# The output projection of a gated mixer as seven block products, with the modulation sums and some weight splits moved

## The chip, the cores and the metric

The kernel runs on one core of a Trainium2 chip. Its metric is the device time of one execution in microseconds, the median of several. The engines are TensorE (PE in the profile, PEld its weight loads), VectorE (DVE), ScalarE (ACT), GpSimd (POOL) and SyncE (SP, which here only issues DMAs). Each runs its own instruction stream in order; semaphores join them.

## The reference, cut to what matters

```python
mod = silu(c) @ w_ada + b_ada                       # six vectors of 1024
sh1, sc1, g1, sh2, sc2, g2 = split(mod, 6)
h = rms_norm(x, norm_mix_g) * (1 + sc1) + sh1
b_s, c_s, v_s, v_c, gl_c, gate_br = split(h @ w_in)
y_a = (b_s * causal_dwconv3(c_s * v_s)) @ w_short_out              # mixer A
u = silu(layer_norm(causal_dwconv31(v_c * sigmoid(gl_c)) + b))
y_b = u @ w_conf_out                                               # mixer B
g_a, g_b = split(sigmoid(gate_br), 2)
mix = (g_a * y_a + g_b * y_b) @ w_o                                # the output projection
x = x + g1 * mix
h2 = rms_norm(x, norm_ffn_g) * (1 + sc2) + sh2
a, bgate = split(h2 @ w_ffn_in, 2)
x = x + g2 * ((silu(a) * bgate) @ w_ffn_out)
return rms_norm(x, final_norm_g)
```

x is 1024 tokens by 1024 channels in float32, the ffn 2816 wide.

## The kernel before

Everything is held transposed: a tile has 128 channels on the partitions and 512 tokens (a "half", `H`) along the row; eight such blocks (`KC`) are the model width. Float32 products are made in three passes: each operand is split into a high part, rounded to the matmul's input form (`copy` on ScalarE), and a low part (the difference, on VectorE or GpSimd); `mm3` then issues high x high, high x low and low x high. For a weight block of 128 x 1024, `split_w` makes both parts (`wh`, `wl`); its argument `lo_engine` says which engine makes the low one.

All large products but one are made by a seven-product block scheme (Winograd's form of Strassen's): the matrices are cut two by two, in channels of the input, pairs of output blocks and halves of the tokens, and `PRODUCTS = "1265734"` names the seven products in the order in which their results can be summed in PSUM. A unit (`dual`) has four output blocks. `product` issues one product of a dual: two PSUM banks, four row blocks, three passes, 24 matmuls. Its operands are sums of blocks: of the activations (made by VectorE and split again) and of the weights (made by VectorE, by GpSimd, or by a DMA that adds into SBUF, `accum_op`).

The stages in order: the first projection with the short convolution and the long one of 31 taps (VectorE's `conv`, whose taps are laid between the evacuations); mixer A's projection (`ya_order`); mixer B's (`CONF_ORDER`), after its layer norm; the output projection `mix`; the ffn in (`in_order`); the ffn out. Weights come through a list `plan`; `next_w` keeps `AHEAD = 2` more loaded and split than the product that is being issued. The order of the instructions on an engine is worked out when the kernel is built, by a planner that goes by costs of its own; `tc.issue_after(ins)` puts an instruction behind another on its engine.

The output projection alone is plain. Weights are whole output columns, `w_o[k]`; for each half, all eight outputs are made one after the other, each with eight row blocks (`col_block`). `mg` holds the split merged activations, `mg_split(j, h)`. Each result is multiplied by g1 and added to x (`scalar_tensor_tensor`, line 1471), stored to DRAM for later (`x1_dram`), squared on ScalarE (1475) and summed (1481). After half 0, `norm_2_first` makes its norm and the eight operands of the ffn's products 1 and 2 (`h2_of`), while half 1 is projected. The second half's norm (`norm_2_start`) is taken in the middle of the ffn's first product, and `norm_2_half` makes its operands beside the next four.

The modulation vectors are 48 sums, each over a block of `w_ada` of 128 x 1024, by one VectorE instruction (`modulation_of`, line 486). Sixteen are made at the start. Of the other 32, fourteen lie in the first projection, two in each of seven duals, through weight buffers; ten are made beside the output projection, by `load_b`; eight beside the ffn.

```python
        for n in range('55'.count(m) * (BEGUN < d < GATED)):
            with tc.issue_after(short_conv.ins):
                modulation_of(MOD_FROM + n_mod, load(ada[MOD_FROM + n_mod], home=...))
```

The second ffn dual, `in_units[1]`, is begun early: `begin` loads its blocks and makes two sums of them (lines 278 and 284) during the output projection, at the places `S2_AT`.

Of the kernel before, what the change touches and what calls it, by code (L numbers as in the profile page):

```python
# [38 lines left out]
ALU = mybir.AluOpType  # L39
# [48 lines left out]

AHEAD = 2


S2_AT = (2, 3, 4)

# [46 lines left out]
def block_kernel(ctx: ExitStack, tc: tile.TileContext, x0, xT, c, vecs, ada, w_first, w_plain, w_duals,  # L140
# [26 lines left out]
    ucp, diffp = (p for _, p in phase_1)  # L167
    rawbp = pool("raw_b", 2, side="right")

    def ps_tile(name):  # L170
# [80 lines left out]
    def dual_units(mats, n, early=0, eng=nc.vector):  # L251
# [20 lines left out]
        def begin():  # L272

            with tc.issue_after(load.ins):
                get("21", "22")
            yield
            with tc.issue_after(parts.lo):
                eng.tensor_tensor(a["22"], a["21"], a["22"], ALU.add)
            with tc.issue_after(load.ins):
                get("11")  # L280
            yield
            a["s2"] = s2p.tile([P, T], F32, tag="x1", name="s2")[:, :n]
            with tc.issue_after(mix.half_0):
                eng.tensor_tensor(a["s2"], a["11"], a["22"], ALU.add)
            yield

        def unit_begun(m):
            get(*{"1": ("11",), "2": ("12",), "5": ("21", "22"), "7": ("11", "12"), "4": ("22",)}.get(m, ()))
            if m == "5":
                sums("1")  # L290
            elif m == "7":
                sums("3")
                eng.tensor_tensor(a["12"], a["12"], a["s2"], ALU.add)
            return split_w(a[{"1": "11", "2": "12", "6": "s2", "5": "s1", "7": "21", "3": "12", "4": "22"}[m]], n, (), eng)
# [61 lines left out]
    def added_units(mats):  # L356
# [9 lines left out]
        def unit(m):  # L366
# [10 lines left out]
            else:  # L377
                raw = a["s1"] if m == "5" else load(mat[{"1": "11", "2": "12", "4": "22"}[m]])
            return split_w(raw, 1024)

        return {m: (lambda m=m: unit(m)) for m in PRODUCTS}

    conf_homes, conf_adds = [rawp, rawbp, rawp], []

    def conf_units(mats, d):
# [15 lines left out]
        def unit(m):  # L401
# [11 lines left out]
            else:  # L413
                raw = get({"1": "11", "2": "12", "4": "22"}[m])
            return split_w(raw, 1024, () if m in "12" else (split.act, split.ins))

# [45 lines left out]
    plan += [yb_units[d][m] for d, m in yb_order]  # L462
    plan += [(w_o[k], 1024) for ks in (range(KC), SECOND[KEPT:]) for k in ks]
    ready = []
# [778 lines left out]
    win_evacs = begun + [win_evac(d, PAIRS[2 * d : 2 * d + 2], win_banks[d]) for d in range(BEGUN, n_duals)]  # L1243
    n_mod = 0
    for d, m in win_order:
# [20 lines left out]
        if win_order.index((d, m)) >= len(win_order) - 7:  # L1266
            q_steps.pop(0)()
        for n in range('55'.count(m) * (BEGUN < d < GATED)):
            with tc.issue_after(short_conv.ins):
                modulation_of(MOD_FROM + n_mod, load(ada[MOD_FROM + n_mod], home=(dual_units.home,dual_units.home)[n_mod % 2]))  # L1270
            n_mod += 1
    while late:
        late.pop(0)()

    tz = {m: [None] * KH for m in PRODUCTS}
# [35 lines left out]

    def load_b(i):

        loaded.append((i, load(ada[i])))
        if len(loaded) > 1:
            with tc.issue_after(split.ins):
                modulation_of(*loaded.pop(0))


    for j in range(KC):  # L1320
        conv(j)
        add_conv(j)
    ma = {}
    loaded = []

# [44 lines left out]
    for i, (d, m) in enumerate(ya_order):  # L1370
        gates_a(d, m)
        product(ya_banks[d], m, tq[m], ya_evacs[d], onto="2")
        if q_steps:
# [12 lines left out]
    mg = [[None, None] for _ in range(KC)]  # L1386

    def mg_split(o, h):
        mg[o][h] = split(ma[o, h], hl_tile, f"mg{o}{h}")

    def yb_evac(d, banks):
# [3 lines left out]
        def out(i, row, h, op, src):  # L1395
# [3 lines left out]
            if (row, h) == (1, 0):  # L1399
                nc.vector.tensor_tensor(ma[j, h], ma[j, h], g, ALU.add)  # L1400
                mg_split(j, h)
            else:
                nc.gpsimd.dma_start(ma[j, h], g, accum_op=ALU.add)
# [38 lines left out]
    def z_3(k):  # L1442
# [5 lines left out]
        (0, "6"): each(z_3, *range(KH)), (1, "6"): each(z_7, *range(KH)), (0, "3"): each(z_4, *range(KH)),  # L1448
        (0, "4"): lambda: [mg_split(j, 0) for j in range(0, KC, 2)],
    }  # L1450
    for d, m in yb_order:
# [4 lines left out]
        product(yb_banks[d], m, tz[m], yb_evacs[d], onto="2", by_k=m in "12")  # L1456
        z_steps.get((d, m), lambda: None)()


    x1 = [None] * KC  # L1460
    x1_dram = [dram.tile([P, T], F32, name=f"x1_dram{j}") for j in range(KC)]

    def mix(i, h):
        j = SECOND[i] if h else i
        xr = g_tile("xr")
        nc.gpsimd.dma_start(xr, xT[j, :, halves[h]])
        (o,) = col_block((second_w if h else first_w)(i), mg, (h,), "mix", SECOND if h else [*range(0, KC, 2), *range(1, KC, 2)])
        if h == 0:
            x1[j] = ucp.tile([P, T + CK - 1], F32, tag="uc", name=f"x1{j}")[:, :T]
        dst = x1[j][:, halves[h]]  # L1470
        evac = nc.vector.scalar_tensor_tensor(out=dst, in0=o, scalar=modc(16 + j), in1=xr, op0=ALU.mult, op1=ALU.add)
        if (i, h) == (KC - 1, 0):
            mix.half_0 = evac.ins
        nc.gpsimd.dma_start(x1_dram[j][:, halves[h]], dst)
        sq = nc.scalar.activation(xr, dst, AF.Square, scale=1.0 / 32.0)
        if (i, h) == (KC - 1, 1):
            load_rsqrt(sq.ins)
        if i == 0:
            sums[h] = xr
        else:  # L1480
            mix.add = nc.vector.tensor_tensor(sums[h], sums[h], xr, ALU.add).ins

    def h2_of(k, h, r2, hi_lo=None):
# [3 lines left out]
        if hi_lo:  # L1487
            hi, lo = hi_lo
            nc.scalar.activation(hi, t, AF.Identity, bias=modc(24 + k))
            nc.vector.scalar_tensor_tensor(  # L1490
                out=lo, in0=t, scalar=modc(24 + k), in1=f32(hi), op0=ALU.add, op1=ALU.subtract
            )
        nc.scalar.activation(t, t, AF.Identity, bias=modc(24 + k))
# [4 lines left out]
    def norm_2_first():  # L1498

        ss, hl = ps_tile("ss"), parts(sums[0])  # L1500
        load_rsqrt(parts.ins)
# [40 lines left out]
    in_units = [dual_units([w_fi[d, m] for m in range(4)], 1024, EARLY[d]) for d in range(N_IN)]  # L1542
    close(phase_1.pop())
    s2p = open_pool("s2", 1, side="right", stack=ctx)[1]
    sums = {}
    for h in range(2):
        for i in range(KC):
            mix(i, h)
            if h == 0:
                mg_split(i, 1)  # L1550
                for b in [32 + i] + [MOD_FROM + n_mod + i] * (MOD_FROM + n_mod + i < 32):
                    load_b(b)
            if (h, i) == (0, KC - 1):
                modulation_of(*loaded.pop())
            if h == 1 and i == 0:
                for k in range(KC):
                    affine(aff2, k, 32, vec, V_GFFN)
                norm_2_first()
            if h == 1 and i in S2_AT:
                next(in_units[1]["begin"])  # L1560


    in_order = [(0, "1"), (0, "2"), (1, "1"), (1, "2"), (2, "1")] + [(d, m) for d in range(2) for m in PRODUCTS[2:]]
# [16 lines left out]

    plan += [lambda d=d, m=m: in_unit(d, m) for d, m in in_order]
    ha = {}
    in_banks = [{} for _ in range(N_IN)]
# [108 lines left out]

    in_product(0, "1", norm_2_start)
    r2 = rstd_end(*r2)
    for i, (d, m) in enumerate(in_order[1:5]):
        norm_2_half(i, r2)
        in_product(d, m)
# [308 lines left out]
```

## Time and profile before

| what | us |
|---|---|
| median of 3 runs (1442.38 to 1443.21) | 1442.85 |
| the profiled execution | 1443.7 |
| its span, first to last instruction | 1441.9 |
| TensorE busy | 1428.6 |
| VectorE busy | 1198.8 |
| ScalarE busy | 655.2 |
| GpSimd busy | 522.0 |

The profile gives, for one execution, the busy time of each engine, the chain of work that ended last, the costliest groups of instructions, and, asked by stretch of time, the busy time of each engine in each stretch. A group's row reads: line, engine, operation, output<-inputs by the program's names, shapes, count | busy us, mean ns of one | idle time ahead of them and what ended it. A row of the timeline begins with its start and its duration in us, and may stand for several like instructions in a row (x4).

### The profile page before, as it was taken

How to read it: one execution, taken by the hardware profiler on the slowest of the kernel's cores; microseconds unless marked ns; L12 is line 12 of the kernel's file. 1: busy time of each engine (PE TensorE's matmuls, PEld its weight loads, DVE VectorE, ACT ScalarE, POOL GpSimd, SP SyncE). 2: the span in 40 equal slices, each digit the busy share in tenths (PEclk: the TensorE clock that was granted, in tenths of full speed). 3: DMA queues.
4: the chain of work that ended last, by engine and by line, in shares of the span. 5: the costliest groups of instructions: out<-in, count | busy, mean ns of one | idle time of the engine just before them, and what ended most of it. 6: DMA issues, size and time to landing. Idle time of an engine off the chain costs nothing.

```text
span 1441.9 us, 17770 instructions
## 1 busy us (share of the span) xinstructions
PE 1428.6 (99%) x6322; PEld 1173.5 (81%) x6322; DVE 1198.8 (83%) x1665; ACT 655.2 (45%) x963; POOL 522.0 (36%) x512
## 2 busy tenths in 40 slices
PE   8999999999999999999999999999999999999997
PEld 4888888888888888888888888888888888888887
DVE  7996999999899999989988898877777665866676
ACT  4873333333343457567426474533444443321235
POOL 0017777777677562013311001110111015563405
PEclk9999999999999999999999999999999999999999
DMA  9743233333335578768886248645555449996903
GB/s 349 282 162 90 72 117 117 103 117 103 132 124 183 161 244 296 219 193 203 223 317 228 79 141 267 205 149 186 185 175 161 138 143 358 389 372 191 340 0 117
DMA packets 95946, 275.04 MB, mean 191 GB/s; under 512 B 10945, under 2 KB 12993, under 8 KB 95858
## 3 DMA queue, kind: packets, MB, share of 16 engines
q1 hardware_dynamic: 46672, 148.92, 30.6%
q0 software_dynamic: 44000, 111.36, 25.6%
q10 hardware_dynamic: 5186, 13.64, 2.5%
q8 instruction: 49, 0.80, 0.2%
q14 instruction: 39, 0.32, 0.1%
HBM read 203.09 MB, written 67.63 MB: 188 GB/s over the span
## 4 chain that ended last, share of the span: by engine, by line
PE 97%; POOL 1%; DVE 0%; issue 0%; POOLq 0%
PE bank L506 14%; PE bank L505 14%; PE bank L508 14%; PE x L508 8%; PE x L506 8%; PE x L505 8%; PE z L506 4%; PE z L508 4%; PE z L505 4%; PE y L508 3%; PE y L506 3%; PE y L505 3%; PE mix L506 2%; PE mix L508 2%; PE mix L505 2%; PE lead L501 1%
## 5 line engine op out<-in xcount | busy, mean ns | idle before, releaser
L244 ACT CAST wh<-raw 128x1024 fp32r<-128x1024 f32 (+2 forms) x254 | 263.0, 1037 | 394.7 <-PE bank L506 138.1
L245 DVE TENSOR_TENSOR wl<-raw,wh 128x1024 fp32r<-128x1024 f32 (+2 forms) x176 | 212.4, 1208 | 38.1 <-ACT wh L244 35.5
L245 POOL TENSOR_TENSOR wl<-raw,wh 128x1024 fp32r<-128x1024 f32 x78 | 194.4, 2500 | 91.1 <-ACT wh L244 90.1
L1168 DVE SCALAR_TENSOR_TENSOR c<-diff,vec,c 128x512 f32<-128x512 f32 x232 | 163.4, 749 | 1.5
L1644 POOL DMA_DIRECT2D hid<-stage x70 | 37.4, 535 | 343.3 <-DVE stage L554 326.8
L505 PE MATMUL bank<-th,wh 128*128 128x512 f32 x336 | 130.7, 389 | 0.0
L506 PE MATMUL bank<-tl,wh 128*128 128x512 f32 x336 | 130.7, 389 | 0.0
L508 PE MATMUL bank<-th,wl 128*128 128x512 f32 x336 | 130.7, 389 | 0.0
L505 PEld LDWEIGHTS bank<-th,wh 128*128 128x128 f32 x336 | 63.1, 188 | 13.2
L508 PEld LDWEIGHTS bank<-th,wl 128*128 128x128 f32 x336 | 63.1, 188 | 13.1
L506 PEld LDWEIGHTS bank<-tl,wh 128*128 128x128 f32 x336 | 63.1, 188 | 13.0
L553 ACT CAST stage<-g 128x512 fp32r<-128x512 f32 x60 | 37.3, 622 | 74.7 <-DMA hid<-stage 41.0
L506 PE MATMUL x<-tl,wh 128*128 128x512 f32 x176 | 68.5, 389 | 0.0
L505 PE MATMUL x<-th,wh 128*128 128x512 f32 x176 | 68.5, 389 | 0.0
L508 PE MATMUL x<-th,wl 128*128 128x512 f32 x176 | 68.4, 390 | 0.0
L1168 DVE SCALAR_TENSOR_TENSOR c<-u,wsum,c 128x512 f32<-128x512 f32 x96 | 66.8, 750 | 0.8
L554 DVE TENSOR_TENSOR stage<-g,stage 128x512 fp32r<-128x512 f32 x60 | 41.2, 688 | 27.9 <-ACT stage L553 27.7
L1668 POOL DMA_DIRECT2D th<-hid x77 | 41.1, 534 | 52.2 <-PE x L508 26.4
L1668 POOL DMA_DIRECT2D tl<-hid x77 | 41.2, 535 | 19.6 <-DMA tl<-hid 5.6
L265 DVE TENSOR_TENSOR raw<-raw 128x1024 f32<-128x1024 f32 (+1 forms) x15 | 17.8, 1188 | 36.4 <-DMA raw<-in_w_fi 24.1
L486 DVE CUSTOM_DVE_ANT_0 raw<-raw,cs,vec 128x1024 f32<-128x1024 f32 x24 | 39.1, 1639 | 9.5 <-DMA raw<-in_ada 5.4
L505 PE MATMUL bank<-t2h,wh 128*128 128x512 f32 x112 | 43.6, 389 | 0.0
(833 smaller groups left out, 4143.1 us busy)
## 6 DMA issues: line engine op xcount, KB each, us to landing
hid<-stage POOLq DMA_DIRECT2D x70, 512.0 KB, 4.8
raw<-in_w_duals SPq DMA_DIRECT2D x65, 512.0 KB, 3.6
raw<-in_w_fi SPq DMA_DIRECT2D x54, 512.0 KB, 4.3
th<-hid POOLq DMA_DIRECT2D x77, 256.0 KB, 6.0
tl<-hid POOLq DMA_DIRECT2D x77, 256.0 KB, 6.0
ada<-in_ada SPq DMA_DIRECT2D x24, 512.0 KB, 5.9
raw<-in_ada SPq DMA_DIRECT2D x24, 512.0 KB, 4.7
raw<-in_w_fo SPq DMA_DIRECT2D x16, 512.0 KB, 6.1
```

Source lines behind the costliest of these rows:

```text
L244: hi = nc.scalar.copy(wh, raw)
L245: lo = lo_engine.tensor_tensor(wl, raw, f32(wh), ALU.subtract)
L265: eng.tensor_tensor(a["s1"], a["21"], a["22"], ALU.add)
L486: nc.vector.tensor_tensor_reduce(out=raw, in0=raw, in1=cs, scale=1.0, scalar=col(V_ADA, b), op0=ALU.mult, op1=ALU.add, accum_out=modc(b),)
L505: nc.tensor.matmul(ps, wh, xh, start=first, stop=False, skip_group_check=again)
L506: nc.tensor.matmul(ps, wh, xl, start=False, stop=False, skip_group_check=again)
L508: mm3.ins = nc.tensor.matmul(ps, wl, xh, start=False, stop=last, skip_group_check=again).ins
L553: t_split.act = nc.scalar.copy(hi, src).ins
L554: t_split.ins = nc.vector.tensor_tensor(lo, src, f32(hi), ALU.subtract).ins
L1168: tap.ins = nc.vector.scalar_tensor_tensor(out=out, in0=src[:, s : s + H], scalar=wt, in1=acc, op0=ALU.mult, op1=ALU.add).ins
L1644: nc.gpsimd.dma_start(hid_dram[key], s)
L1668: nc.gpsimd.dma_start(t, hid_dram[key][:, s])
```

## The change

Five things change together.

1. The output projection is made by seven block products for each of two duals, in the order `MIX_ORDER`. Its weights are loaded as blocks (`mix_units`), sums of blocks by adding DMAs on GpSimd's queue. Its operands are block sums of the merged activations (`m_6`, `m_7`, `m_4`) and plain blocks, split by `tm_split`. Evacuations add g1 times a product, or minus that, into x1. Mixer B's order `CONF_ORDER` is changed so that the blocks needed first come first.
2. With it, `norm_2_first` is issued between the two banks of product 5 of the second dual; `norm_2_start` after the ffn's second product; `norm_2_half` goes with three products instead of four. Shifts of the first half's operands (`shift_2`) go behind the second norm's start.
3. The fourteen modulation sums of the first projection become 28 half sums, one every third product, through a half-size buffer of their own. The next ten leave the output projection: one in every two products of mixer A and B, through the buffer of the convolution's differences.
4. Low parts of weights on GpSimd instead of VectorE: products 1, 2, 4 and 5 of mixer B (`LO_POOL`), and products 1 and 2 of the first three ffn duals.
5. The two sums of `begin` go to GpSimd, at other places (`S2_AT`); of the second half's sums of squares, some.

```diff
-S2_AT = (2, 3, 4)
+LO_POOL = {"ya": "", "yb": "1245", "mix": ""}
+S2_AT = (0, "5"), (1, "5"), (0, "3")
-CONF_ORDER = [(d, m) for m in "1256" for d in range(2)] + [(0, "3")] + [(d, m) for m in "74" for d in range(2)] + [(1, "3")]
-MOD_FROM = 16
+CONF_ORDER = [(d, m) for m in "1256" for d in range(2)] + [(0, "3"), (0, "7"), (0, "4"), (1, "7"), (1, "4"), (1, "3")]
+MIX_ORDER = [(d, m) for m in "1267453" for d in range(2)]
+MOD_FROM, MOD_WIN, MOD_LAST, MOD_EVERY = 16, 14, 24, 3
...
         def begin():
-            with tc.issue_after(parts.lo):
-                eng.tensor_tensor(a["22"], a["21"], a["22"], ALU.add)
+            nc.gpsimd.tensor_tensor(a["22"], a["21"], a["22"], ALU.add)
...
-            with tc.issue_after(mix.half_0):
-                eng.tensor_tensor(a["s2"], a["11"], a["22"], ALU.add)
+            nc.gpsimd.tensor_tensor(a["s2"], a["11"], a["22"], ALU.add)
...
-                w = split_w(a["1" + m], n, (), eng)
+                w = split_w(a["1" + m], n, (), nc.gpsimd if early else eng)
...
+    def mix_units(mats, d):
+        def add(raw, b):
+            conf_adds.append(nc.gpsimd.dma_start(raw, mat[b], accum_op=ALU.add).ins)
+        def unit(m):
+            if m == "6":
+                raw = a["s2"] = get("11", "21", "22", home=(rawp, rawbp)[d])
+            elif m == "3":
+                raw = a["s2"]
+                add(raw, "12")
+            else:
+                raw = get(*{"1": ("11",), "2": ("12",), "7": ("21", "11"), "4": ("22",), "5": ("22", "21")}[m])
+            return split_w(raw, 1024, (split.act, split.ins), lo_engine("mix", m))
...
+    def half_modulation(behind, every=1):
+        n_step += 1
+        if n_step % every or n_mod >= 2 * MOD_WIN:
+            return
+        i, h = n_mod // 2, n_mod % 2
+        with tc.issue_after(load.ins):
+            nc.sync.dma_start(half_ada, ada[MOD_FROM + i][:, halves[h]])
+        n_mod += 1
+        half_sums(i, h, behind)
...
+    def late_modulation(step, behind):
+        if step % 2 == 0:
+            if whole:
+                with tc.issue_after(behind):
+                    modulation_of(MOD_FROM + n_mod, whole.pop())
+                n_mod += 1
+        elif n_mod < MOD_LAST:
+            whole.append(diffp.tile([P, T + CK - 1], F32, tag="diff", name="ada")[:, :T])
+            with tc.issue_after(load.ins):
+                nc.sync.dma_start(whole[0], ada[MOD_FROM + n_mod])
...
+            row, h = {"2": (0, 0), "6": (0, 1), "3": (0, 1), "7": (1, 1), "5": (1, 1), "4": (1, 0)}[m]
+            j = 4 * d + 2 * i + row
+            dst = x1[j][:, halves[h]]
+            src = dst if m in "53" else xrs.pop((j, h))
+            ins = nc.vector.scalar_tensor_tensor(
+                out=dst, in0=ps, scalar=ngm[:, j : j + 1] if row else modc(16 + j), in1=src, op0=ALU.mult, op1=ALU.add
+            ).ins
...
+        steps = {
+            (0, "2"): each(m_6, 0, 1), (1, "2"): each(m_6, 2, 3), (0, "6"): each(m_7, *range(KH)),
+            (1, "6"): each(m_4, *range(KH)), (0, "7"): lambda: [tm_split("5", k, b[0, 0][k]) for k in range(KH)],
+            (0, "4"): lambda: [tm_split("3", k, b[1, 1][k]) for k in range(KH)],
+        }
+        for d, m in MIX_ORDER:
+            xr_loads(d, m)
+            product(banks[d], m, tm[m], evacs[d], norm_2_first if (d, m) == (1, "5") else None, onto="2")
...
-    in_product(0, "1", norm_2_start)
+    in_product(0, "1")
+    in_product(0, "2")
+    with tc.issue_after(mm3.ins):
+        norm_2_start()
```

More of the change, by code (lines that the diff above doesn't have):

```diff
@@ L168, in block_kernel @@
     rawbp = pool("raw_b", 2, side="right")
+    halfp = open_pool("half", 1, side="right")
+    half_ada = halfp[1].tile([P, H], F32, tag="half", name="half_ada")
+    half_sum = halfp[1].tile([P, 1], F32, tag="sum", name="half_sum")
     def ps_tile(name):
@@ L1267, in block_kernel @@
             q_steps.pop(0)()
[L1268 to L1271, printed above, removed]
+        half_modulation(reads[-1][1], MOD_EVERY)
     while late:
         late.pop(0)()
+    assert n_mod == 2 * MOD_WIN, n_mod
+    def late_modulation(step, behind):
+        nonlocal n_mod
+        if step % 2 == 0:
+            if whole:
+                with tc.issue_after(behind):
+                    modulation_of(MOD_FROM + n_mod, whole.pop())
[4 more added lines that the diff above has]
+                nc.sync.dma_start(whole[0], ada[MOD_FROM + n_mod])
+    whole, n_mod = [], MOD_WIN
     tz = {m: [None] * KH for m in PRODUCTS}
@@ L1457, in block_kernel @@
         z_steps.get((d, m), lambda: None)()
+        late_modulation(len(ya_order) + yb_order.index((d, m)), split.ins)
     x1 = [None] * KC
     x1_dram = [dram.tile([P, T], F32, name=f"x1_dram{j}") for j in range(KC)]
[L1463 to L1469, printed above, removed]
+    sums, xrs = {}, {}
@@ L1470, in mix, with xr_loads, x1_done @@
+    def xr_loads(d, m):
+        row, h = {"2": (0, 0), "6": (0, 1), "7": (1, 1), "4": (1, 0)}.get(m, (0, None))
+        for i in range(2 * (h is not None)):
+            j = 4 * d + 2 * i + row
+            xrs[j, h] = g_tile("xr")
+            with tc.issue_after(conf_adds[-1]):
+                nc.gpsimd.dma_start(xrs[j, h], xT[j, :, halves[h]])
+    def x1_done(j, h, sq, ins):
         dst = x1[j][:, halves[h]]
-        evac = nc.vector.scalar_tensor_tensor(out=dst, in0=o, scalar=modc(16 + j), in1=xr, op0=ALU.mult, op1=ALU.add)
@@ L1498, in norm_2_first @@
     def norm_2_first():
-        ss, hl = ps_tile("ss"), parts(sums[0])
+        ss, hl = ring[1][0], parts(sums[0])
         load_rsqrt(parts.ins)
@@ L1542, in block_kernel @@
     in_units = [dual_units([w_fi[d, m] for m in range(4)], 1024, EARLY[d]) for d in range(N_IN)]
-    close(phase_1.pop())
+    close(phase_1.pop(), halfp)
     s2p = open_pool("s2", 1, side="right", stack=ctx)[1]
[L1545 to L1560, printed above, removed]
     in_order = [(0, "1"), (0, "2"), (1, "1"), (1, "2"), (2, "1")] + [(d, m) for d in range(2) for m in PRODUCTS[2:]]
@@ L1581, in block_kernel @@
     plan += [lambda d=d, m=m: in_unit(d, m) for d, m in in_order]
+    ngm = cp.tile([P, KC], F32, name="ngm")
+    nc.vector.tensor_scalar(ngm, mod[:, 16:24], -1.0, None, ALU.mult)
+    for k in range(KC):
+        affine(aff2, k, 32, vec, V_GFFN)
+    for d, m in mix():
+        if (d, m) in S2_AT:
+            next(in_units[1]["begin"])
+    raws[:] = [rawp] * 3 + [rawbp] * 2
     ha = {}
```

125 lines of the change are left out of this document (95 added, 30 removed).

## The prediction

> **What bounds the kernel now.** I read the page's first two parts, then the chain, then the busy times by stage.
>
> ```profile
> span 1441.9 us, 17770 instructions
> PE 1428.6 (99%) x6322; PEld 1173.5 (81%) x6322; DVE 1198.8 (83%) x1665; ACT 655.2 (45%) x963; POOL 522.0 (36%) x512
> PEclk9999999999999999999999999999999999999999
> PE 97%; POOL 1%; DVE 0%; issue 0%; POOLq 0%
> ```
>
> TensorE is busy for 99% of the span at the full granted clock, and the chain that ended last is 97% TensorE. So a matmul that is taken away shortens the run by its own step, as long as nothing else becomes late. The table by stage shows which engine would: short conv and convolution (64 to 561), the two branch projections (564 to 643 mixer A, 643 to 711 mixer B), the output projection (711 to 802), the start of the ffn (802 to 830), and a stretch of plain ffn.
>
> ```profile
> core 0: us, PE busy (x) PEld busy (x) DVE busy (x) ACT busy (x) POOL busy (x), PEclk, DMA share, GB/s
> 64.00:300.00 236.00, 236.00 (x1043) 195.39 (x1042) 211.91 (x307) 105.75 (x153) 150.09 (x78) 1.00 0.34 113
> 300.00:500.00 200.00, 200.00 (x884) 165.62 (x883) 190.01 (x274) 77.84 (x109) 138.15 (x71) 1.00 0.42 140
> 500.00:561.00 61.00, 61.00 (x271) 50.52 (x270) 59.45 (x85) 34.20 (x55) 33.15 (x15) 1.00 0.80 253
> 564.00:643.00 79.00, 79.00 (x349) 64.96 (x348) 69.38 (x101) 45.37 (x68) 8.31 (x11) 1.00 0.78 223
> 643.00:711.00 68.00, 68.00 (x299) 55.55 (x298) 66.02 (x97) 43.45 (x67) 18.57 (x25) 1.00 0.79 196
> 711.00:802.00 91.00, 91.00 (x402) 75.12 (x401) 72.91 (x109) 41.15 (x60) 19.67 (x35) 1.00 0.74 258
> 802.00:830.00 28.00, 28.00 (x123) 22.81 (x123) 24.49 (x33) 14.24 (x21) 0.00 (x0) 1.00 0.22 62
> 900.00:1200.00 300.00, 300.00 (x1325) 248.42 (x1324) 221.20 (x275) 132.71 (x195) 35.76 (x67) 1.00 0.53 173
> ```
>
> TensorE has no gap in any of them. VectorE (DVE) is the second limit: 97% busy in 643 to 711 and 500 to 561, 88% in 564 to 643 and 802 to 830, but only 80% in 711 to 802. GpSimd (POOL) is nearly empty from 564 on.
>
> **The matmuls removed.** The same table restricted to the tile `mix`:
>
> ```profile
> 705.00:806.00 101.00, 87.39 (x384) 72.07 (x384) 12.00 (x16) 1.00 0.75 250
> ```
>
> The projection is 8 outputs x 2 halves x 8 row blocks x 3 passes = 384 matmuls in 87.39 us, 0.2276 us each; the ffn stretch gives 300/1325 = 0.2264. Seven block products are 7 x 2 x 2 x 4 x 3 = 336. So 48 fall away: 48 x 0.2264 = 10.9 us. One product is 24 matmuls, 5.44 us, and the fourteen take 76.2 us. This term is sure; everything else is what of it is lost again.
>
> **VectorE in the new projection.** Durations that I need:
>
> ```profile
> L245 DVE TENSOR_TENSOR wl<-raw,wh 128x1024 fp32r<-128x1024 f32 x14 | 17.1, 1221 | 0.5 <-ACT wh L244 0.3
> L486 DVE CUSTOM_DVE_ANT_0 raw<-raw,cs,vec 128x1024 f32<-128x1024 f32 x10 | 12.7, 1281 | 0.0
> L486 DVE DVE_READ_ACCUMULATOR2_ANT mod<- 128x1 f32 x10 | 0.8, 84 | 0.0
> L1471 DVE SCALAR_TENSOR_TENSOR x<-mix,mod,xr 128x512 f32<-128x512 f32 x16 | 12.0, 750 | 12.3 <-PE mix L508 12.3
> L1481 DVE TENSOR_TENSOR xr<-xr 128x512 f32<-128x512 f32 x14 | 9.6, 689 | 3.0 <-ACT xr L1475 3.0
> 534.15 2.49 DVE L1101 TENSOR_TENSOR q<-q,q1h 128x512 fp32r<-128x512 f32 x4
> ```
>
> The ten modulation sums leave the stage: -10 x (1.28 + 0.08) = -13.6 us. Evacuations go from 16 to 24 (products 2, 6, 7, 4, 5, 3 of two duals and two banks; product 1 goes to ScalarE): +8 x 0.75 = +6.0. Operands: 5 products x 4 splits and 16 block sums, where 8 splits of the second half were before: +28 x 0.62 (four in 2.49 us) = +17.4. One more weight: +1.2. Three sums of squares go to GpSimd: -2.1. The first ffn weights' low parts (three in this stage) and two sums of the begun unit go there too: -5 x 1.22 = -6.1. Together 72.9 + 2.8 = 75.7 us of 80.1 that remain of the 91. It fits, with 4.4 us free instead of 18; the five instructions that move to GpSimd take most of that again if each blocks VectorE for 1 us (below), which is why the edges get a price. ScalarE (41 us plus 12 splits and 4 copies of 0.62, as its cast quoted further down) stays far below. The loads of x and the stores of x1 stay sixteen each.
>
> **The sums moved ahead.** Ten whole sums now lie in 564 to 700, one in two products: six in mixer A's stage, +6 x 1.36 = 8.2 on 69.4 of 79 us: full, but not over. Four lie in mixer B's, +5.4 on 66.0 of 68; eight of that stage's low parts leave VectorE, -8 x 1.22 = -9.8. So by its own work mixer B's stage falls to 61.6. The earlier fourteen become 28 halves, one in three products over the whole first projection. No row shows a half; nearest is a whole one at 1.28, so 0.64 + 0.08 bare, and the blocking below on top. The fourteen take 39.1 - 12.7 = 26.4 us now, 1.89 each:
>
> ```profile
> L486 DVE CUSTOM_DVE_ANT_0 raw<-raw,cs,vec 128x1024 f32<-128x1024 f32 x24 | 39.1, 1639 | 9.5 <-DMA raw<-in_ada 5.4 <-issue 4.0
> 544.38 3.01 POOL L1199 TENSOR_TENSOR tot<-tot,u 128x512 f32<-128x512 f32 x2 [0.72 <-DVE u L1168]
> 560.89 1.88 PE L1208 MATMUL mu<-tot,ones 128*128 128x512 f32 x4
> ```
>
> That is 0.61 above the 1.28. With 0.61 on each half, 28 x 1.33 = 37 us replace 28 us (26.4 and the reads): 9 us more, against 36 us in which VectorE idles from 64 to 561, though the last 60 us have only 1.5. There the cover is another: the channel sums are done at 547.4 and TensorE takes them at 560.9, 13.5 us later. I count 0.5 us for this and mixer A's stage, bounds 0 and 9.
>
> **Low parts on GpSimd.** One costs 2.50 us there for 1.22 on VectorE. The rows in which the two engines meet:
>
> ```profile
> L245 POOL TENSOR_TENSOR wl<-raw,wh 128x1024 fp32r<-128x1024 f32 x78 | 194.4, 2500 | 91.1 <-ACT wh L244 90.1
> L433 DVE TENSOR_TENSOR raw<-raw x4: 3030/3049/3252, 433.7 to 511.9; 128x1024 f32<-128x1024 f32 x4
> L265 DVE TENSOR_TENSOR raw<-raw 128x1024 f32<-128x1024 f32 x13 | 15.9, 1223 | 31.2 <-DMA raw<-in_w_fi 24.1 <-DMA raw<-in_w_fo 7.1
> 534.84 4.08 POOL L245 TENSOR_TENSOR wl<-raw,wh 128x1024 fp32r<-128x1024 f32 x1 [2.28 <-ACT wh L244]
> L1168 DVE SCALAR_TENSOR_TENSOR c<-diff,vec,c 128x512 f32<-128x512 f32 x232 | 163.4, 749 | 1.5
> ```
>
> An add of two SBUF tiles took 3.05 us beside a GpSimd add where the same form takes 1.22 alone: 1.83 of blocking. But in the other direction GpSimd's 2.5 us became 4.08 while VectorE ran its four q splits (534.15, above) back to back; and the taps, one input of which lies in PSUM, keep 749 ns throughout. [...]
>
> So the price hangs on one number, the blocking b that each low part puts on VectorE. Bounds: 0 (GpSimd falls into VectorE's waits and PSUM reads) and 2.5. The nearest rows give 0.61 (sums) and 1.83 (L433); mixer B's stage is mostly SBUF operands, packed closely, which lets GpSimd wait, so I take 1.0. Then the stage has 61.6 + 8 x 1.0 = 69.6 us of VectorE work in 68; some of it has slack before its reader, so I count 1.0 us of stall.
>
> **Edges of the projection.** At its start the last merged block is added by a DMA, 3.2 to 8.2 us to landing; it is first needed by product 6, four products or 21.8 us in:
>
> ```profile
> DMA to landing us min/median/max: 3.2/6.1/8.2
> 757.20 0.62 ACT L682 CAST sumh<-xr 128x512 fp32r<-128x512 f32 x1 [0.76 <-DVE xr L1481]
> 770.62 0.76 DVE L1490 SCALAR_TENSOR_TENSOR h23l<-x,mod,h23h 128x512 fp32r<-128x512 f32 x1
> 801.77 1.12 PE L695 MATMUL ss<-xr,ones 128*128 128x512 f32 x2
> 830.28 0.69 DVE L554 TENSOR_TENSOR t2l<-t,t2h 128x512 fp32r<-128x512 f32 x1 [0.69 <-ACT t2h L553]
> ```
>
> Evacuation 1.5, landing 8.2 and four operands of some 2.5 us make 20: it fits, so nothing. At its end the cover shrinks. The first half's norm, from its cast to the fourth operand, took 771.4 - 757.2 = 14.2 us and had 42 us before the ffn's first product, whose middle the ss row marks (801.8 - 2.7 - 757.2); now it starts in the middle of the twelfth product, with 2.5 products or 13.6 us left. The second half's norm took 801.8 to 831.0, five products; it now starts after the second ffn product, with three (16.3 us) and what product 6 gives before it reads the last operand. Its bare VectorE work is 8 x 0.75 + 12 x 0.69 + 2.1 = 16.4 us; low parts that stood between go to GpSimd. Late next would be that fourth operand. I count 2.0 us for both places, bounds 0 (the freed VectorE time covers it) and 8 (16.4 + 1.8 until the root is there + 2 x 0.69 and 2 x 1.22 of other VectorE work + 2 x 1.0 of blocking = 24, against 16.3, if product 6 gave nothing); nearer to 0, since five such products show no TensorE gap today with VectorE at 88%.
>
> **Transfers.**
>
> ```profile
> L398 POOL DMA_DIRECT2D raw<-in_w_conf x6 | 5.7, 944 | 46.0 <-DVE rl0t L570 19.8 <-DVE z2l L546 11.3 <-DVE bank L867 8.6
> ```
>
> Blocks are loaded 22 times (10 of them added by GpSimd's queue) instead of 13: +4.7 MB in the stage, while ten modulation blocks, 5.2 MB, leave it. Mixer A's stage takes 3.1 MB on 17.6 (223 GB/s x 79 us): share 0.78 to some 0.92. Weights are fetched two products (10.9 us) ahead, which hides a late landing; a stage over 1.0 would not be hidden. SyncE's queue carries the moved loads in turn; nothing else waits on it. GpSimd issues 10 more accumulating DMAs of 0.94 us as in the row, beside 20 us busy of 91; behind them on its queue wait the loads of x, needed only by an evacuation of the same product. I count 0.
>
> **Sum.** -10.9 + 0.5 + 1.0 + 2.0 = -7.4. The profiled execution took 1443.7 (span 1441.9 and 1.8 around it): 1436.3. The median shown, 1442.85, is 0.85 below it, so 1435.5.
>
> **Rivals.**
> - *All of it comes out:* VectorE's freed time covers every edge. For it: not one gap in today's stages at 97% VectorE. 1443.7 - 10.9 - 0.85 = 1432.
> - *VectorE becomes the bound:* b is 1.83 as in L433. Mixer B's stage: 61.6 + 14.6 = 76.2 in 68, 8.2 lost; the edges lose their 2: 1442.85 - 10.9 + 10.2 = 1442. Against it: GpSimd's 4.08 us row, where it was GpSimd that waited.
> - *The low parts on GpSimd make it slower:* b is the whole 2.5. Mixer B's stage then holds 61.6 + 20 = 81.6 in 68, 13.6 us lost: 1442.85 - 10.9 + 13.6 = 1445.6, 1447.6 with the edges. It decides from b = (68 + 10.9 - 61.6)/8 = 2.16 on, or 1.9 with the edges' 2 us. Only L433 comes near.
>
> **How the numbers follow.** Runs of this kernel differ by 0.06%; about 0.2% (2.9 us) is what can be told from no change. Forecast, one to seven us of stalls, 1433 to 1439: 0.57. All of it out: 0.15. VectorE the bound: 0.15. Slower: 0.13. The first two are faster, 0.72; the third the same, 0.15; the last slower, 0.13. The range leaves out a tenth on either side: 1431.5 to 1445. The likeliest case's own range is 1433 to 1439.
>
> **What would show it.** 336 matmuls of the projection where 384 were; VectorE's share over 90% in it; VectorE adds of two SBUF tiles longer than 1.3 us between 620 and 720 only where a GpSimd low part runs (b is their excess per low part); TensorE gaps at the start of the ffn, released by h2 or t2 operands. Wrong it would be if TensorE waits in the first projection (for half sums or late evacuations), or for a merged block at product 6.

## The result, and the profile after

The changed kernel takes 1487.06 us (median of 4 runs, 1484.26 to 1489.74) against 1442.99 before: ratio 1.0306, 95% interval 1.0286 to 1.0325. It is 44 us slower, where 7.4 us faster was predicted. The profiled execution took 1486.74, 43.0 more than that of before. The page's first parts and the head of its chain:

```profile
span 1485.0 us, 17811 instructions
PE 1435.7 (97%) x6274; PEld 1171.3 (79%) x6274; DVE 1246.7 (84%) x1712; ACT 663.7 (45%) x980; POOL 576.5 (39%) x541
PE 74%; DVE 11%; DMA 5%; issue 3%; POOL 3%; ACT 2%; SPq 0%; POOLq 0%; ACTq 0%; DVEq 0%
```

The 48 matmuls are gone (6322 to 6274). But the chain, which was 97% TensorE, is 74% now, and every other engine has a share of it. The table by stage says where. With gapless TensorE a matmul took 0.2264 us, so a stage's length less its matmul count times 0.2264 is what TensorE lost there.

```profile
300.00:500.00 200.00, 198.80 (x877) 164.16 (x876) 191.55 (x282) 76.92 (x108) 138.65 (x69) 1.00 0.42 135
500.00:535.00 35.00, 28.61 (x119) 23.24 (x118) 32.37 (x41) 11.31 (x17) 19.93 (x11) 0.90 0.52 154
569.00:643.00 74.00, 70.02 (x295) 55.89 (x294) 66.11 (x99) 42.52 (x65) 6.28 (x6) 0.98 0.84 263
643.00:735.00 92.00, 80.95 (x336) 63.93 (x336) 88.98 (x121) 49.28 (x74) 41.38 (x40) 0.96 0.77 202
735.00:775.00 40.00, 34.45 (x140) 27.60 (x139) 24.09 (x36) 13.85 (x21) 12.84 (x18) 0.91 0.91 209
775.00:829.00 54.00, 53.19 (x236) 43.72 (x235) 49.28 (x63) 27.80 (x41) 24.61 (x29) 1.00 0.82 261
829.00:875.00 46.00, 37.38 (x142) 27.82 (x140) 44.21 (x53) 26.87 (x43) 11.61 (x8) 0.89 0.27 80
```

Lost: 1.4 and 8.1 in the first projection, 7.2 in mixer A, 15.9 in mixer B and the merge, 8.3 at the start of the output projection and 0.6 in its rest, 13.9 at the start of the ffn. Together 55.4; less the 10.9 of the matmuls that is 44.5, against 43.0 measured. So the count closes to 1.5 us, and the loss lies at five places: the first projection, mixer A, mixer B, the start of the output projection and the start of the ffn. TensorE's waits (line, releaser: us in total, times, longest) name who was late:

```profile
PE bank L542 <- ACT wh L249: 6.4, 1, 6.4
PE bank L542 <- ACT bank L1559: 5.5, 2, 4.3
PE ss L732 <- DVE sq L1550: 5.1, 1, 5.1
PE bank L543 <- DVE z2l L583: 4.0, 1, 4.0
PE x L543 <- DVE h22l L1623: 2.5, 1, 2.5
```

**First projection.** Four engines in the timeline of the changed kernel (start, us, engine; in brackets the idle time ahead and what ended it):

```profile
501.86 5.03 POOL L250 TENSOR_TENSOR wl<-raw,wh 128x1024 fp32r<-128x1024 f32 x2
502.22 5.23 DVE L1299 CUSTOM_DVE_ANT_0 half_ada<-half_ada,cs,vec 128x512 f32<-128x512 f32 x1
507.49 5.29 SPq L1291 DMA_DIRECT2D half_ada<-in_ada  x2
512.87 0.60 SPq L233 DMA_DIRECT2D raw<-in_w_duals  x1
524.31 0.33 SPq L942 DMA_DIRECT2D sig<-part  x1
528.12 0.59 ACT L945 COPY bank<-sig 128x512 f32<-128x512 f32 x1 [7.99 <-DMA sig<-part]
```

A half sum stood 5.23 us on VectorE beside two low parts of GpSimd (another one, at 511.67, took 0.75). There is one buffer for halves, so the load of the next half can be issued only after the sum of the one before: SyncE was held until the late half sum had ended, and then for 5.29 us more over two such loads. A weight load and the loads of `part` stood behind them. (Between the two loads of `part` SyncE waited 9.2 us for a weight buffer; in e3, below, it waits there too, 7.9 us.) ScalarE waited 7.99 us for the second load of `part`, its weight cast behind that, and TensorE 6.4 us for the cast.

**Mixer A.** No single wait of TensorE is long there:

```profile
PE bank L545 <- DVE wl L250: 2.2, 1, 2.2
PE y L542 <- ACT y L1403: 1.8, 1, 1.8
```

Behind the wait of 2.2 us the granted clock fell (0.98 in the mean over the stage, 0.66 from 605 to 610).

**Mixer B.** VectorE and GpSimd:

```profile
664.14 2.82 POOL L250 TENSOR_TENSOR wl<-raw,wh 128x1024 fp32r<-128x1024 f32 x1 [3.44 <-ACT wh L249]
664.62 3.49 DVE L1355 TENSOR_TENSOR cv<-cv,rl1r 128x512 f32<-128x512 f32 x2
667.82 2.49 POOL L250 TENSOR_TENSOR wl<-raw,wh 128x1024 fp32r<-128x1024 f32 x1 [0.86 <-ACT wh L249]
668.03 2.82 DVE L583 TENSOR_TENSOR z2l<-cv,z2h 128x512 fp32r<-128x512 f32 x1
679.60 2.40 POOL L250 TENSOR_TENSOR wl<-raw,wh 128x1024 fp32r<-128x1024 f32 x1 [0.25 <-ACT wh L249]
679.62 3.46 DVE L523 CUSTOM_DVE_ANT_0 ada<-ada,cs,vec 128x1024 f32<-128x1024 f32 x1
```

A `cv` or `z2l` instruction takes 0.68 us without company and a whole sum 1.28. Here they took 3.49 for two, 2.82 and 3.46: each of these three GpSimd low parts held VectorE for about 2.2 us. Not each of the eight does; e7, below, has the mean.

**Start of the output projection.** GpSimd's queue and the VectorE instruction that needs it:

```profile
749.48 1.29 POOL L1468 DMA_DIRECT2D ma<-gb  x1
756.45 0.88 POOL L441 DMA_DIRECT2D raw<-in_w_o  x1 [5.68 <-DMA raw<-in_w_o]
758.09 0.69 DVE L595 SCALAR_TENSOR_TENSOR t2m<-ma,ma 128x512 f32<-128x512 f32 x1 [11.39 <-DMA ma<-gb]
758.91 0.89 POOL L1468 DMA_DIRECT2D ma<-gb  x1
```

The merged blocks are added by DMAs (`ma<-gb`) on that queue. Between two of them stands the add of a weight block, which may be issued only when the block under it has landed: 5.68 us. Loads of x on the same queue waited 3.49 and 3.96 us (at 741.80 and 747.82) for an add to leave a buffer. VectorE is idle for 11.39 us.

**Start of the ffn.** The last sum of squares, on which the second norm hangs:

```profile
845.24 4.65 POOL L250 TENSOR_TENSOR wl<-raw,wh 128x1024 fp32r<-128x1024 f32 x2
845.30 5.15 DVE L1550 TENSOR_TENSOR sq<-sq 128x512 f32<-128x512 f32 x1 [0.31 <-ACT sq L1543]
```

It took 5.15 us, and 0.68 at 844.31: again 2.2 us for each low part.

### The profile page after: what moved, and what is told of

Its sections match the earlier page's. It is cut to its first block, busy times and chain, and to the rows that moved or that the text cites. A ratio compares the mean times of both kernels' runs of the same rounds, so it can differ in the third digit from the quotient of the medians.

```text
span 1485.0 us, 17811 instructions
## 1 busy us (share of the span) xinstructions
PE 1435.7 (97%) x6274; PEld 1171.3 (79%) x6274; DVE 1246.7 (84%) x1712; ACT 663.7 (45%) x980; POOL 576.5 (39%) x541
## 4 chain that ended last, share of the span: by engine, by line
PE 74%; DVE 11%; DMA 5%; issue 3%; POOL 3%; ACT 2%; SPq 0%; POOLq 0%; ACTq 0%; DVEq 0%
PE bank L543 10%; PE bank L542 10%; PE bank L545 10%; PE x L542 8%; PE x L543 8%; PE x L545 8%; PE z L542 4%; PE z L545 4%; PE z L543 4%; PE y L542 2%; PE y L545 2%; PE y L543 2%; DMA ma<-gb 2%; PE lead L538 1%; DVE wl L250 1%
## 5 line engine op out<-in xcount | busy, mean ns | idle before, releaser
L250 POOL TENSOR_TENSOR wl<-raw,wh 128x1024 fp32r<-128x1024 f32 x92 | 228.7, 2493 | 129.8 <-ACT wh L249 129.7
L250 DVE TENSOR_TENSOR wl<-raw,wh 128x1024 fp32r<-128x1024 f32 (+2 forms) x163 | 197.8, 1214 | 34.1 <-ACT wh L249 32.5
L545 PEld LDWEIGHTS bank<-th,wl 128*128 128x128 f32 x336 | 63.5, 189 | 13.3
L543 PEld LDWEIGHTS bank<-tl,wh 128*128 128x128 f32 x336 | 63.5, 189 | 13.1
L523 DVE CUSTOM_DVE_ANT_0 ada<-ada,cs,vec 128x1024 f32<-128x1024 f32 x34 | 44.9, 1345 | 0.0
```

The costliest lines, as they stand in the source:

```text
L250: lo = lo_engine.tensor_tensor(wl, raw, f32(wh), ALU.subtract)
L523: nc.vector.tensor_tensor_reduce(out=raw, in0=raw, in1=cs, scale=1.0, scalar=col(V_ADA, b), op0=ALU.mult, op1=ALU.add, accum_out=modc(b),)
L543: nc.tensor.matmul(ps, wh, xl, start=False, stop=False, skip_group_check=again)
L545: mm3.ins = nc.tensor.matmul(ps, wl, xh, start=False, stop=last, skip_group_check=again).ins
```

## The experiments

The first four start from the changed kernel and undo one thing each; the next two undo several; two more start from the kernel before and do one thing each; the last two ask what the ten late sums and the adding DMAs cost.

**e1: mixer B's low parts back on VectorE**

```diff
-LO_POOL = {"ya": "", "yb": "1245", "mix": ""}
+LO_POOL = {"ya": "", "yb": "", "mix": ""}
```

> The changed kernel, with mixer B's low parts of products 1, 2, 4 and 5 back on VectorE. The changed kernel takes 1487; its matmuls lose some 16 us from 643 to 735, mixer B's stage and its edge. Theory: there VectorE's two-SBUF instructions stand still while a GpSimd low part runs (2.0 to 2.9 us for one of 0.68). Then the eight that come back cost VectorE 9.8 us and free it of some 15: the stage loses 6 to 10 instead of 16, 1477 to 1481. Rival: VectorE has simply too much work there with four modulation sums more; then 9.8 us more of work makes it worse, 1490 to 1497.

1480.58 us, ratio 1.0265 (1.025 to 1.028): 6.5 less. Mixer B and the merge lost 6.4 us of TensorE (92 - 378 x 0.2264) where it was 15.9; but the projection after it lost more, with VectorE idle for 17.5 us on a merged block. So the low parts cost more there than the VectorE time that they save, and part of the cure is spent at the next place.

**e2: the ffn's low parts, `begin`'s sums and the sums of squares back on VectorE**

```diff
-return split_w(..., n, (), nc.gpsimd if m in "12" else eng)
+return split_w(..., n, (), eng)
-            nc.gpsimd.tensor_tensor(a["22"], a["21"], a["22"], ALU.add)
+            eng.tensor_tensor(a["22"], a["21"], a["22"], ALU.add)
...
```

> The changed kernel, with the low parts of the first three ffn duals, the two sums of the begun dual and the three sums of squares back on VectorE. Its matmuls lose 14 us from 829 to 875, at the start of the ffn. Theory: the norm's operands are held up by GpSimd (a sum of squares took 5.15 us, one scaling 2.85 instead of 0.74); with everything on VectorE the stage loses 4 to 8, 1477 to 1481. Rival: the norms have been moved to where there is too little time, whoever makes the low parts; then the 12 us of work that come back make it no better: 1486 to 1495.

1480.16 us, ratio 1.0263 (1.0246 to 1.028): 6.9 less. The wait for `sq` fell from 5.1 to 1.9 us.

**e3: the first projection's fourteen sums whole, as before**

```diff
-        half_modulation(reads[-1][1], MOD_EVERY)
+        for n in range('55'.count(m) * (BEGUN < d < GATED)):
+            with tc.issue_after(short_conv.ins):
+                modulation_of(MOD_FROM + n_mod, load(ada[MOD_FROM + n_mod], home=...))
```

> The changed kernel, with the fourteen sums of the first projection whole again and where they were. Its matmuls lose 10 us from 300 to 535, 8.5 of them after one wait of 6.5 at 523. Theory: both halves go through one buffer, so the second half's load waits on SyncE's queue for the first half's sum, which a GpSimd low part held up for 4.5 us; behind it stood the load of a weight block. Without halves the 10 us go: 1476 to 1478. Rival: VectorE is late there because a half costs almost as much as a whole; then the wait would come back only in part, 1480 to 1485, and if it is chance of the order, 1485 to 1489.

1474.05 us, ratio 1.0217 (1.0201 to 1.0232): 13.0 less, more than expected. The 6.4 us wait is gone; SyncE issued the second load of `part` 10.4 us earlier than in the changed kernel:

```profile
513.86 0.37 SPq L942 DMA_DIRECT2D sig<-part  x1
```

Mixer A's loss went too, from 7.2 to 1.9 us, though nothing of mixer A was edited. The half sums are not shown to be its cause: e1 and e4 keep them and lose only 3.1 and 2.5 there.

**e4: own buffers for the loads of x**

```diff
-            xrs[j, h] = g_tile("xr")
+            xrs[j, h] = s_tile("xr")
```

> The changed kernel, with the projection's tiles of x taken from the large pool of operands instead of the six buffers of the gates. Its matmuls lose 8.6 us from 758 to 775, where VectorE waits 11.4 and 2.9 us for the DMA that adds mixer B's last blocks. Theory: the loads of x wait on GpSimd's queue for a gate buffer that is free only when such an add has landed, and the next add stands behind them, so the adds go one after the other; with tiles of their own they go at once: 1478 to 1481. Rival: the adds are late because mixer B is late or the DMA engines are full; then 1485 to 1489.

1488.01 us, ratio 1.0308 (1.0291 to 1.0325): nothing gained in all. The loads of x no longer wait for a buffer, and TensorE lost 4.5 us from 735 to 775 (40 - 157 x 0.2264) instead of 8.3; but the stretch behind it, 775 to 829, lost 8.3 instead of 0.6. And the first add still stands behind a weight block's, so VectorE waits for it no shorter than before:

```profile
748.20 0.86 POOL L441 DMA_DIRECT2D raw<-in_w_o  x1 [6.93 <-DMA raw<-in_w_o]
748.73 1.22 POOL L1468 DMA_DIRECT2D ma<-gb  x1
755.05 0.69 DVE L595 SCALAR_TENSOR_TENSOR t2m<-ma,ma 128x512 f32<-128x512 f32 x1 [13.12 <-DMA ma<-gb]
```

**e5: e1, e2 and e3 together, and the second half's merged blocks added by VectorE**

```diff
-            if (row, h) == (1, 0):
+            if (row, h) == (1, 0) or h == 1:
                 nc.vector.tensor_tensor(ma[j, h], ma[j, h], g, ALU.add)
```

> The changed kernel with all low parts and begun sums back on VectorE, the fourteen sums whole as before, and the merged blocks of the second half added by VectorE instead of a DMA on GpSimd's queue. What stays of the change: seven products, the ten sums ahead, the norms later. One by one the first three gave 6.5, 6.9 and 13.0 us. Theory: they are separate losses and add up, 1487 - 26.4 = 1460.6, and the wait of VectorE for the merging DMAs (11 us of TensorE's time with mixer B faster) goes too: 1450 to 1456. Rival: the waits only move from one edge to the next; then 1465 to 1475.

1452.61 us, ratio 1.0067 (1.005 to 1.0083). Of 44 us, 34.5 are gone, by four edits that leave the seven products and the ten moved sums. The largest of the waits left:

```profile
PE bank L542 <- DVE vz L904: 3.2, 1, 3.2
```

**e6: e5 without the ten late sums.** Their blocks are neither loaded nor summed; the columns of the modulation that they make hold 0.25.

```diff
-    whole, n_mod = [], MOD_WIN
+    whole, n_mod = [], MOD_LAST
+    nc.gpsimd.memset(mod[:, ...], 0.25)
```

> As the version with everything back, and the ten modulation blocks beside mixer A and B are neither loaded nor summed (their columns are filled with a constant, so the output is another). Theory: ten sums of 1.36 us in stages whose VectorE is 88% and 97% busy cost 5 to 10 us of TensorE's time: that much below the version with everything back. Rival: they fill waits of VectorE and cost nothing: within 2 us of it.

1447.65 us, ratio 1.0034 (1.0021 to 1.0047): 5.0 us less than e5, where the runs of each spread over some 4 us. In the table below, from one execution of each, mixer A and B lose 9.0 us less and the stages after them 6.7 more, 2.1 us net for these two: the loads and sums of the ten blocks cost most of TensorE's loss in the mixers, and much of the gain is spent behind them. Even without them the projection by seven products does not pay. The largest wait left, the stretch around it, and the same stretch of the projection in e5:

```profile
PE bank L726 <- ACT sumh L719: 3.4, 1, 3.4
765.00:790.00 25.00, 20.33 (x76) 15.99 (x75) 16.63 (x23) 10.47 (x15) 3.29 (x7) 0.86 0.66 207
771.74 1.05 ACT L249 CAST wh<-raw 128x1024 fp32r<-128x1024 f32 x1 [7.20 <-DMA raw<-in_w_o]
730.00:790.00 60.00, 59.91 (x265) 49.27 (x264) 52.19 (x74) 30.43 (x46) 18.17 (x30) 1.00 0.89 255
```

The first three rows are of e6, the last is of e5. L726 is the first norm's matmul, which now stands in the middle of product 5; the product's second bank stands behind it and waits with it: in e6 the norm's two matmuls start at 780.29 and 782.03, the second bank's first at 782.63. Its place alone is not the cause: e5 has the norm at the same place and lost nothing from 730 to 790. In e6 ScalarE, which makes `sumh`, had stood 7.20 us at the cast of a block of `w_o` before; in e5 it stood 2.28 us, for a block that landed at about the same time (its cast began at 772.35), and e6 lost 25 - 76 x 0.2264 = 7.8 us in its row.

**e7: the kernel before, with only mixer B's eight low parts on GpSimd**

```diff
-return split_w(raw, 1024, () if m in "12" else (split.act, split.ins))
+return split_w(raw, 1024, () if m in "12" else (split.act, split.ins), nc.gpsimd if m in "1245" else nc.vector)
```

> The kernel before, with one edit: mixer B's low parts of products 1, 2, 4 and 5 on GpSimd. The kernel before has no TensorE gap there. Theory (GpSimd's low parts stop VectorE's two-SBUF instructions): 4 to 12 us slower, 1447 to 1455, and instructions of 0.68 us that take 2 to 3. Rival (they free VectorE of 9.8 us): 1443 or less.

1452.54 us, ratio 1.0066 (1.0051 to 1.0081): this edit alone costs 9.2 us. Its stage and its waits:

```profile
632.00:672.00 40.00, 33.60 (x138) 26.12 (x137) 38.00 (x48) 23.84 (x36) 24.61 (x20) 0.96 0.71 180
```

```profile
PE bank L505 <- ACT z1h L545: 3.1, 1, 3.1
PE bank L506 <- DVE z5l L546: 2.4, 1, 2.4
```

40 - 138 x 0.2264 = 8.8 us are lost in these 40, behind operands that VectorE delivers late. Single instructions were held for up to 2.2 us here too (a `z2l` of 0.68 took 2.90 and another 2.88), others for less. Over the whole run VectorE's busy time gives the mean:

```profile
PE 1432.3 (99%) x6322; PEld 1174.8 (81%) x6322; DVE 1203.4 (83%) x1657; ACT 653.7 (45%) x963; POOL 543.8 (37%) x520
```

It has eight instructions fewer than before and yet rose from 1198.8 to 1203.4: (4.6 + 8 x 1.22) / 8 = 1.8 us of holding for each low part.

**e8: the kernel before, with only the 28 half sums**

```diff
+    half_ada = halfp[1].tile([P, H], F32, tag="half", name="half_ada")
...
-        for n in range('55'.count(m) * (BEGUN < d < GATED)):
...
+        half_modulation(reads[-1][1], MOD_EVERY)
```

> The kernel before, with one edit: the fourteen sums of the first projection as 28 halves through one half-size buffer. Theory (the second half's load blocks SyncE's queue ahead of the weight blocks): 8 to 13 us slower, 1451 to 1456, with a long TensorE wait where a weight block came late. Rival (only the changed kernel's order met it): within 3 us of before.

1452.64 us, ratio 1.0064 (1.0049 to 1.0079): 9.3 us, and the same picture as in the changed kernel:

```profile
508.18 5.28 SPq L1257 DMA_DIRECT2D half_ada<-in_ada  x2
513.56 0.40 SPq L231 DMA_DIRECT2D raw<-in_w_duals  x1
```

```profile
PE bank L508 <- ACT wh L247: 6.1, 1, 6.1
```

**e9: e5 with all 24 sums whole in the first projection**, four in each of its duals until they are used up.

```diff
+        for n in range('5577'.count(m) * (BEGUN < d < GATED) * (n_mod < MOD_LAST)):
```

> As the version with everything back (1452.6), and the ten sums beside mixer A and B moved further ahead, into the first projection, whole and four a dual, where VectorE idles for 34 us from 64 to 500. Theory: there they cost nothing, as if they were left out: 1446 to 1449. Rival: sums beside GpSimd's low parts there are held up and take weight buffers: 1452 or more.

1462.82 us, ratio 1.0133 (1.0118 to 1.0148): worse than e5: the theory failed, and the time lies in the rival's range, though not for the rival's reason alone, since the sums themselves were seldom held up (median 1.29 us, longest 3.09). The convolution shares VectorE with them and ends later (its taps still run at 571 us, where the kernel before had the channel sums done at 547.4), and TensorE waits for the channel sums that come from it:

```profile
PE mu L1245 <- POOL tot L1236: 6.4, 1, 6.4
```

**e10: e9 with the merged blocks added by DMA again**, as in the changed kernel.

> As the version with 24 sums in the first projection, but the merged blocks of the second half added by DMAs on GpSimd's queue again, as in the changed kernel. Theory: on that queue each add stands behind loads and weight adds that wait for a landing, so product 6 of the projection waits for its operand again: 4 to 11 us more than with VectorE adding. Rival: the adds were late only because mixer B was; then no more, or less by the 5 us of VectorE work saved.

1474.75 us, ratio 1.0219 (1.0202 to 1.0236): 11.9 more than e9, most of it at the start of the projection: 13.1 us of TensorE's time are lost from 735 to 775 (40 - 119 x 0.2264), none in e9. GpSimd's queue there:

```profile
721.95 1.24 POOL L1471 DMA_DIRECT2D ma<-gb  x1
730.44 0.86 POOL L441 DMA_DIRECT2D raw<-in_w_o  x1 [7.25 <-DMA raw<-in_w_o]
732.73 0.86 POOL L1471 DMA_DIRECT2D ma<-gb  x1
741.57 1.10 POOL L1541 DMA_DIRECT2D xr<-in_xT  x2 [7.42 <-DMA ma<-gb]
743.23 1.30 POOL L1471 DMA_DIRECT2D ma<-gb  x1
```

One merged block in 10.8 and in 10.5 us (in the changed kernel, 7.0 and 9.4 at this place): each add has ahead of it on the queue a load that waits for a landing, now a weight block's, now the merged block's before it.

All of it in one table: TensorE's loss by stage, worked out as above (the stages' bounds follow each kernel's own times), and its sum, less 10.9 where the projection has seven products, beside what the profiled execution took over that of before (1443.7). In e9 and e10 the first projection ends later, so its column runs to 600 us and the next two are one.

| kernel | first projection | mixer A | mixer B, merge | projection, ffn start | sum, net | measured |
|---|---|---|---|---|---|---|
| changed | 9.5 | 7.2 | 15.9 | 22.8 | 44.5 | 43.0 |
| e1 | 9.7 | 3.1 | 6.4 | 28.6 | 37.0 | 36.6 |
| e2 | 7.1 | 7.7 | 14.6 | 17.9 | 36.4 | 35.5 |
| e3 | 0.1 | 1.9 | 13.3 | 27.0 | 31.4 | 30.7 |
| e4 | 10.2 | 2.5 | 15.0 | 25.0 | 41.8 | 40.2 |
| e5 | 0.0 | 2.3 | 9.1 | 6.4 | 6.9 | 7.4 |
| e6 | 0.0 | 0.0 | 2.4 | 13.1 | 4.6 | 5.3 |
| e7 | 0.0 | 0.0 | 8.8 | 0.0 | 8.8 | 8.6 |
| e8 | 10.2 | 0.0 | 0.0 | 0.0 | 10.2 | 9.6 |
| e9 | 14.3 | 2.3 | with A | 10.5 | 16.2 | 15.2 |
| e10 | 18.1 | 0.5 | with A | 23.9 | 31.6 | 30.8 |

A loss taken away at one place comes back in part at a later one (e1, and e6's 13.1), so single undoings don't add up to the whole; e5's do better because they go together.

## Why the prediction was wrong

- *Matmuls, -10.9:* right, 48 fewer.
- *Half sums and mixer A, +0.5 of 0 to 9:* mis-sized. The half sums alone measure 9.3 (e8); the changed kernel lost 9.5 in the first projection, and 7.2 in mixer A, which the half sums don't explain (e1, e4 and e8 have them and lose 3.1, 2.5 and nothing there). The step counted VectorE's microseconds against its idle time. The cost was not there but in "SyncE's queue carries the moved loads in turn; nothing else waits on it": the half's load with its one buffer was put ahead of weight loads and the loads of `part`, and e8 shows 5.28 us on that queue for two of these loads. This step failed outright; the change added a wait on a queue, and what stood behind that wait was not looked up.
- *Low parts in mixer B, +1.0 with b = 1.0:* mis-sized, 9.2 in e7. The rows of low parts that got in first show up to 2.2 us, and the mean over e7's eight is 1.8. The nearest row with the right shape, L433's 1.83, was right; the choice of 1.0 rested on the sums' 0.61 and on GpSimd's 4.08 us row, where GpSimd was the one to wait. That row exists again (4.51 us for a low part at 661.47 in e7), but the other four between 631 and 668 got in first (2.40 to 3.09 us). So b is the second rival's, and below the 2.16 from which the third was to lose. The third rival had the direction, slower, but not the reason: no run shows its 2.5, where the rows come to 2.2 and the mean to 1.8, and its 1447.6 leaves out the other losses. That e7 loses with 1.8 shows a second fault, in the way from b to a stall. By the step's own count e7's stage holds 66.0 - 9.8 + 8 x 1.8 = 70.6 us of VectorE work in 68, 2.6 too much, and it lost 8.8: instructions held for up to 2.2 us, whose results TensorE was about to read, stopped TensorE (its waits of 3.1 and 2.4 us there), whatever the sum of the stage left free. In the changed kernel's rows above (3.49 us for two, 2.82, 3.46 and 5.15) the held instructions read two tiles in SBUF, GpSimd's low part had begun 0.02 to 0.48 us before them, and each held them for 2.1 to 2.2 of its 2.3 to 2.8 us.
- *Start of the projection, "it fits, so nothing":* failed. The sum took the landing of one DMA, 8.2 us at most. What counts is the rate of the queue, one merged block in 7.0 to 10.8 us (the changed kernel and e10). "Behind them on its queue wait the loads of x" was looked at, what stands ahead of them was not. Price: 8.3 us here in the changed kernel, 11.9 between e9 and e10.
- *Start of the ffn, inside +2.0 of 0 to 8:* mis-sized, 13.9. "Late next would be that fourth operand" was half right: `h22l` is late by 2.5 us, but the larger wait is the second norm's last sum of squares behind two low parts, and e2, with these back on VectorE, ends 6.9 us earlier.
- *The ten sums in mixer A and B:* "full, but not over" and "by its own work mixer B's stage falls to 61.6" counted them as free. Leaving out their loads and sums takes 9.0 us of loss out of these stages and 5.0 us off the time (e6 against e5), by waits such as the one for `vz`, 3.2 us in e5 and 1.1 in e6. VectorE worked without a gap from a sum at 686.56 to that evacuation at 697.86, so the sum is the likely reason; the loads were not taken away without the sums.
- *The signs named in advance:* both "wrong it would be if" came: waits in the first projection for half sums, and for a merged block at product 6.

What stays open: why mixer A lost 7.2 us in the changed kernel and 7.7 in e2, but 2 to 3 in the other versions with the ten sums (without them, in e6, nothing), beyond this: in these two the clock fell there (0.98 in the mean), in e1 and e4 it did not (1.00); and why e10 lost 8.2 us between 300 and 420 where e9 lost 4.3, when their sources differ only after it. Without mixer B's and the ffn's low parts on GpSimd, half sums, merging DMAs of the second half and late sums (e6) the seven products still lose 15.5 us to gain 10.9: 7.8 where a block of `w_o` is late and the first norm's matmul behind it, 5.2 at the ffn's first products (822 to 875), 2.4 in mixer B. Whether another order of loads or norms would save them was not tried. No version beat the kernel before.

## What to carry to other kernels

A kernel like this one, whose TensorE has no gap while VectorE is 97% busy in places, has little slack to lend: before moving work, look up for every moved DMA what stands behind it on its queue and what it must wait for, and take the queue's rate, not one landing's latency. Work moved from VectorE to another engine is no gain where it holds VectorE up: here 1.22 us were saved for each low part, and 1.8 paid on the mean (e7). And price each part by itself against the stage in which it lands; parts that each looked covered by idle time cost together five times the one sure gain (55.4 us against 10.9).

## What was not expected of the hardware

Behind TensorE's longest waits the granted clock was lower, so that they cost more than their length. The stretch around the first projection's wait, ahead of it and two after it, in the table by stretch of time (the column after the engines is the granted clock):

```profile
522.00:529.00 7.00, 1.37 (x7) 0.79 (x5) 7.00 (x10) 0.88 (x2) 3.94 (x2) 0.84 0.53 176
529.00:534.00 5.00, 4.25 (x11) 3.40 (x12) 5.00 (x9) 1.63 (x2) 3.94 (x3) 0.54 0.04 16
534.00:539.00 5.00, 5.00 (x24) 4.10 (x23) 5.00 (x9) 2.44 (x4) 2.46 (x2) 1.00 0.99 225
```

After 6.4 us of waiting the clock was 0.54 for the next 5 us, whose row has 11 matmuls where the one behind it, with the clock at 1.00, has 24; so the wait cost 8.1 us in all (500 to 535). Likewise e8's wait of 6.1 us cost 8.8 (500 to 540, the clock 0.91 in the mean) and e10's of 10.9 cost 13.1 (735 to 775, 0.83). The wait of 1.2 us between 300 and 500 left the granted clock at 1.00, and so did waits of 1.8 and 1.9 us in the changed kernel (584 to 589 and 715 to 720). Behind its waits of 2.2 us in mixer A and of 2.5 at the start of the ffn the clock was 0.66 (605 to 610 and 833 to 838), behind those of 4.0 and 4.3 us 0.50 (671 to 676 and 767 to 772). In e7 the row with waits of 3.1 and 2.4 us has 0.96 in the mean over 40 us (632 to 672): by that share 1.6 us of clock are missing for the two of them, where the one wait in mixer A took 0.34 x 5 = 1.7. So a single wait of 2.2 us was enough in one place, and one of 1.9 was not in another. The three waits of 6 us and more cost 1.7, 2.7 and 2.2 us above their length; from these an estimate for a forecast is some 2 us on top of such a wait; for one of about 2 us these runs show both.
